# Gate/up blocks of a feed-forward group: two plain blocks replaced, six blocks started with the products that need no token differences

## The chip, the cores and the metric

The kernel runs on one core of one Trainium2 chip. The metric is the device time of one execution in microseconds (us). TensorE (PE) multiplies matrices and writes PSUM, VectorE (DVE) and ScalarE (ACT) work element by element, GpSimd (POOL) does little here, SyncE (SP) issues the loads. Each engine takes its instructions in the order of the built program.

## The reference, cut to what matters

One layer of a transformer step over 640 tokens (128 context, 512 latent) with width 1024. After attention, convolution and the output projection the layer ends in a SwiGLU feed-forward part with 2816 inner columns:

```python
h2 = _rms(x, norm_ffn) * (1 + sc2) + sh2
gate, up = jnp.split(h2 @ w_gate_up, 2, axis=-1)
x = x + g2 * ((jax.nn.silu(gate) * up) @ w_down)
```

All of it is float32.

## The kernel before, in words

**Precision.** Each float32 operand is kept as a high and a low part. `split` (L150) makes the high part on ScalarE and the low part on VectorE; `mm3` (L154) issues three matmuls for each product of two such operands (high x high, high x low, low x high).

**Tiling of gate/up.** The 2816 inner columns are 22 blocks f of 128, in four groups (`GCUT`, 6 + 6 + 5 + 5). For each block there are a gate weight "g" and an up weight "u", both 1024 x 128. A product here means 512 inputs x 128 columns x 320 tokens, 12 matmuls in `prod`. Let A11, A12 be the two input halves of g, A21, A22 those of u, and B11, B21 the two input halves of h2 for the first 320 tokens (LO), B12, B22 for the other 320 (HI). A *plain* block needs 8 products. A block by the Strassen-Winograd scheme needs 7: A11 B11, A12 B21, S1 T1, S2 T2, S3 T3, S4 B22, A22 T4. Here S1 = A21 + A22, S2 = S1 - A11, S3 = A11 - A21, S4 = A12 - S2 are sums of weights, and T1 = B12 - B11, T2 = B22 - T1, T3 = B22 - B12, T4 = B21 - T2 are differences between token halves. Blocks 0 and 1 are plain (`NPLAIN` = 2), all others take 7 products.

**Functions.** `plain` (L1183) runs the 8 products of a plain block: 4 on LO, later 4 on HI. `ff_a` to `ff_e` (L1215 to L1248) run the 7 products of the others: `ff_a` A11 B11, `ff_c` S1 T1, `ff_d` S2 T2, `ff_b` A12 B21, `ff_e` S3 T3, S4 B22, A22 T4. Partial results go from one PSUM bank to another, or to SBUF ("u2", "p5"), by a ScalarE copy. `ff_end` finishes the HI half, `ff_out` splits the result into the tile "gT" for the down product. `down` (L1256) runs a group's down product in two column halves; in group 0 it also runs the steps of the second half of the gate vector g2 (`g2_step`, VectorE) on four loads of w_ada.

**Where the h2 parts come from.** The output projection's loop ends with `h2_turn` (L1006): PE transposes a token block, ScalarE writes it to SBUF. For the last token block this stands inside block 0's products. `b_plain` and `b_put` (L1066) split a part of h2, `b_sums` (L1080) makes T1 to T4 and splits them, in two blocks of tokens of a half (0 to 192 and 192 to 320; before: 128 to 320 and 0 to 128).

**What sets the order.** PE's order is written out by hand. VectorE's order is written out between `dve_order.__enter__` and `__exit__`; instructions from outside may still be put between. All else is placed by a scheduler by priority (`early`). Weights stream through a list: `plan` (L188) puts loads and splits in order, and `W` (L259), called by each product, works that list up to 6 entries ahead (`AOP`). A raw load goes to one of three buffers "wf" (`WFB`), its parts to one of four "wh" and "wl" (`WHB`); a load is issued on SP when its buffer is free. `PRODS` gives the order of a block's splits, `PAIRS` says which tile holds which operand. `SEQ` (L39) is the hand-written order of the attention; in it S, T and O are attention steps, F1 is a piece of convolution, and r0 to r4 are `att_rms` (L952), two small matmuls on a sum that GpSimd has made.

Of the kernel before, what the change touches and what calls it, by code (L numbers as in the profile page):

```python
# [15 lines left out]
P = 128  # L16
# [33 lines left out]
GCUT = [0, 6, 12, 17, 22]  # L50
GB = 3
# [4 lines left out]
AOP = 6  # L56
NPLAIN = 2
PPO = ''
# [33 lines left out]
def build(ctx, tc, x_prompt, x_sample, c, cache_k, cache_v, c_ctx, norm_mix, norm_ffn, w_ada, b_ada,  # L92
# [101 lines left out]
    def op_load(e):  # L194

        f, name = e[0][1:]
        g, u = (order[place[x, f]][5] for x in "gu")
        a11, a12, a21, a22 = g[:, 0:4], g[:, 4:8], u[:, 0:4], u[:, 4:8]
        if name[0] == "S":
            if name == "S12":  # L200
                sums[f] = T("sx", (P, 8, P), F32, 2)
            s13, s24 = sums[f][:, 0:4], sums[f][:, 4:8]
            with early(SOP[f >= NPLAIN]):
                for out, x, y, op in {"S12": ((s13, a21, a22, ALU.add), (s24, s13, a11, ALU.subtract)),
                                      "S34": ((s13, a11, a21, ALU.subtract), (s24, a12, s24, ALU.subtract))}[name]:
                    dve.tensor_tensor(out, x, y, op)
            src = sums[f]
        else:
            src = {"A1": g, "A2": u, "A22": a22}[name]
# [6 lines left out]
        with early(SOP[f >= NPLAIN]):  # L216
            split(*e[5], src)
# [37 lines left out]
    def load_next(later=False):  # L255
        load(order[stream_at[0]], later)
        stream_at[0] += 1

    def W(key):  # L259
        p = place[key]  # L260
        while not in_pre[0] and stream_at[0] < len(order):
            nxt = order[stream_at[0]][0][0]
            ahead = AO if nxt == "o" else AOP if nxt in ("g", "u", "op") else AHEAD
# [28 lines left out]
    PAIRS = {"A11": ("A1", 0), "A12": ("A1", 4), "A21": ("A2", 0), "A22": ("A2", 4),  # L292
             "S1": ("S12", 0), "S2": ("S12", 4), "S3": ("S34", 0), "S4": ("S34", 4)}
# [764 lines left out]
    def b_tile(name):  # L1058
        w = T("gT" if name == "B12" else name, (P, 2, 4, HALF), F32R, GB if name == "B12" else 1)
        B[name] = [(w[:, 0, i], w[:, 1, i]) for i in range(4)] + [w]  # L1060
# [18 lines left out]

    def b_sums(part):  # L1080
        n = part.stop - part.start
# [8 lines left out]
        diff("T2", b22, w["T1"])  # L1090
        b_put("T1", w["T1"], part)
        diff("T3", b22, b12)
        b_put("T2", w["T2"], part)
        diff("T4", b21, w["T2"])
        b_put("T3", w["T3"], part)
        b_put("T4", w["T4"], part)
# [73 lines left out]
    open_pool("Y2", "left", "B22 T1 T2 T3 T4")  # L1170
    open_pool("G", "right", "cg cu p5 u2 dm tr")
    gT, st, pair = {}, {}, [None]
# [4 lines left out]
    def prod(out, f, a, b, start=True, stop=True, more=False):  # L1177
        x, k0 = PAIRS[a] if f < NPLAIN or a != "A22" else (a, 0)
# [4 lines left out]
    def plain(f, bs, toks, mid=None):  # L1183

        ps = [FB(), FB()]
        for x, a in zip(ps, ("A1", "A2")):
            for i in (1, 2):
                if mid is not None and (a, i) == ("A2", 2):
                    mid()
                prod(x, f, f"{a}{i}", bs[i - 1], i == 1, i == 2)  # L1190
        if toks is LO:
            st[f] = T("cg", (P, TOK), F32, 2), T("cu", (P, TOK), F32, 2)
        cg, cu = st[f]
        act.activation(cg[:, toks], ps[0][:, :HALF], AF.Silu)
        dve.tensor_tensor(cu[:, toks], ps[1][:, :HALF], cg[:, toks], ALU.mult)
        if toks is HI:
            ff_out(f, cu)
            del st[f]

# [9 lines left out]
    def copy_of(tag, ps):  # L1209
# [3 lines left out]
        return x  # L1213

    def ff_a(f):  # L1215
        b1, b2 = FB(), FB()
        prod(b1, f, "A11", "B11")
        with early(CPP):
            act.activation(b2[:, :HALF], b1[:, :HALF], AF.Copy)
        st[f] = [b1, b2, T("cg", (P, TOK), F32, 2), None, None, None]  # L1220

    def ff_b(f):
        b2, cg = st[f][1:3]
        prod(b2, f, "A12", "B21", start=False, more=True)
        act.activation(cg[:, LO], b2[:, :HALF], AF.Silu)

# [9 lines left out]
    def ff_e(f):  # L1236
        b1, _, cg, b3, p5, u2 = st[f]
        prod(b1, f, "S3", "T3", start=False, more=True)
        b4 = FB()
        with early(CPP):  # L1240
            act.activation(b4[:, :HALF], b1[:, :HALF], AF.Copy)  # L1241
# [4 lines left out]
        dve.tensor_tensor(cu[:, LO], b4[:, :HALF], cg[:, LO], ALU.mult)  # L1246
        st[f] = cg, cu, b3, u2

    def ff_end(f):
        cg, cu, b3, u2 = st.pop(f)  # L1250
        dve.tensor_tensor(cg[:, HI], b3[:, :HALF], u2, ALU.add)
        act.activation(cg[:, HI], cg[:, HI], AF.Silu)
        dve.tensor_tensor(cu[:, HI], cu[:, HI], cg[:, HI], ALU.mult)
        ff_out(f, cu)

    def down(gi, grp):  # L1256
        last = gi == len(GROUPS) - 1
        blocks = [grp[i:i + 2] for i in range(0, len(grp), 2)]
        for j in range(2):
# [23 lines left out]
            for t in range(NT):  # L1283
                cc = 1 if t == CTX else 0
                for part in acc[t]:
# [7 lines left out]
                    if last:  # L1293
                        sp.dma_start(o_dram[t][:, oc], x2[t][:, oc])

    for gi, grp in enumerate(GROUPS):
        for f in grp:
            if f == 0:
                dve_order = tc.manual_schedule(engines={mybir.EngineType.DVE})
                dve_order.__enter__()  # L1300
                b_plain("B12 B22", slice(0, 192))
                for x in range(NPLAIN):
                    plain(x, ("B11", "B21"), LO, None if x else lambda: h2_turn(TORD[-1], BPL))
                    if x == 0:
                        with early(BPL):
                            b_plain("B12 B22", slice(192, HALF))
                        b_sums(slice(128, HALF))
                        for _ in range(4):
                            load_next()
                b_sums(slice(0, 128))  # L1310
                dve_order.__exit__(None, None, None)
                phase[0] = 3
                for x in range(NPLAIN):
                    plain(x, ("B12", "B22"), HI)
            elif f >= NPLAIN:
                ff_a(f)
                if f - 1 in st and FEND == 1:
                    ff_end(f - 1)
                ff_c(f)
# [3 lines left out]
                ff_b(f)  # L1323
                ff_e(f)
                if f == grp[-1] or FEND == 0:
                    ff_end(f)
        down(gi, grp)
# [54 lines left out]
```

## Time and profile before

| | us |
|---|---|
| median of 3 runs | 755.55 (754.55 to 755.95) |
| the profiled execution | 756.18 |
| its span in the profile | 754.4 |
| VectorE busy | 530.2 (70%) |
| ScalarE busy | 374.9 (50%) |
| gate/up of group 0 in the span | 320.22 to 401.52 |

The span runs from the first to the last instruction in the profile; the execution's own time has 1.8 us around it. A time in a row of the profile counts from the span's start. Busy time of PE does not say that PE works at its peak, since matmuls overlap: their price is read from the step between two starts. The granted clock of TensorE is full over the whole span.

### The profile page before, as it was taken

To read this page: it belongs to the slowest core of one execution; us is meant where nothing else is said; L and a number is where in the kernel's file an instruction comes from. 1 tells how busy PE (TensorE), PEld (TensorE's weight loads), DVE (VectorE), ACT (ScalarE), POOL (GpSimd) and SP (SyncE) were. 2 spreads that over 40 slices of the span, in tenths; PEclk is the share of its full clock that TensorE was granted. 3 is DMA by queue.
4 is the path that set the end of the run, shared out by engine and by line. 5 is a ranking of instruction groups with operands and counts; after the bars stand their busy time and mean duration, and the time that the engine had idled before them with its cause. 6 is when DMAs were issued, how large, how long until landed. Compare 5 with 4: busy or idle time off the path is not lost.

```text
span 754.4 us, 11635 instructions
## 1 busy us (share of the span) xinstructions
PE 732.7 (97%) x4556; PEld 657.7 (87%) x4556; DVE 530.2 (70%) x905; ACT 374.9 (50%) x701; POOL 49.5 (7%) x85
## 2 busy tenths in 40 slices
PE   7999999999989999999899999999999999999997
PEld 5568878988988887899898799999889998899986
DVE  5558878676656798787868768774568766677653
ACT  5356777677666534775552225553125551255510
POOL 2403101011010120100000000000000000000000
PEclk9999999999999999999999999999999999999999
DMA  9985133533522464031225313233112232123312
GB/s 289 288 244 163 45 109 100 167 93 93 173 92 91 133 226 137 1 112 48 87 91 181 113 56 97 72 99 125 56 56 84 84 112 83 45 72 110 99 70 84
DMA packets 101387, 84.50 MB, mean 112 GB/s; under 512 B 3502, under 2 KB 81650, under 8 KB 101332
## 3 DMA queue, kind: packets, MB, share of 16 engines
q1 hardware_dynamic: 100980, 83.39, 35.9%
q0 software_dynamic: 352, 0.37, 0.3%
q8 instruction: 36, 0.59, 0.3%
q14 instruction: 19, 0.16, 0.1%
HBM read 79.68 MB, written 2.75 MB: 109 GB/s over the span
## 4 chain that ended last, share of the span: by engine, by line
PE 78%; DVE 7%; DMA 6%; ACT 5%; issue 2%; SPq 1%; POOL 1%; ACTq 0%; DVEq 0%
PE pf L155 17%; PE pf L156 17%; PE pf L157 17%; PE pc L723 3%; PE pc L724 3%; PE pc L725 3%; PE ps L835 2%; PE po L879 2%; PE pt L862 2%; DMA es<-t 2%; PE pc L394 2%; DMA af<-in_w_ada_dram 2%; DMA wf<-in_w_gate_up_dram 1%; PE ph L156 1%; PE ph L157 1%
## 5 line engine op out<-in xcount | busy, mean ns | idle before, releaser
L152 DVE TENSOR_TENSOR wl<-wf,wh 128x1024 fp32r<-128x1024 f32 (+1 forms) x58 | 68.7, 1185 | 59.1 <-ACT wh L151 44.6
L151 ACT ACTIVATE wh<-wf 128x1024 fp32r<-128x1024 f32 (+1 forms) x68 | 65.6, 968 | 86.2 <-PE pf L157 45.6
L155 PE MATMUL pf<-B,wh 128*128 128x320 f32 x288 | 89.3, 310 | 0.0
L157 PE MATMUL pf<-B,wl 128*128 128x320 f32 x288 | 89.3, 310 | 0.0
L156 PE MATMUL pf<-B,wh 128*128 128x320 f32 x288 | 89.2, 310 | 0.0
L155 PE MATMUL pf<-T,wh 128*128 128x320 f32 x280 | 86.9, 310 | 2.2 <-ACT pf L1241 1.6
L155 PE MATMUL pf<-wh,gT 128*128 128x512 f32 (+1 forms) x225 | 87.0, 387 | 0.0
L157 PE MATMUL pf<-T,wl 128*128 128x320 f32 x280 | 86.7, 310 | 0.0
L156 PE MATMUL pf<-T,wh 128*128 128x320 f32 x280 | 86.7, 310 | 0.0
L156 PE MATMUL pf<-wl,gT 128*128 128x512 f32 (+1 forms) x225 | 86.6, 385 | 0.0
L157 PE MATMUL pf<-wh,gT 128*128 128x512 f32 (+1 forms) x225 | 86.6, 385 | 0.0
L151 ACT ACTIVATE wh<-sx 128x1024 fp32r<-128x1024 f32 x40 | 42.4, 1060 | 82.9 <-PE pf L157 49.8
L152 DVE TENSOR_TENSOR wl<-sx,wh 128x1024 fp32r<-128x1024 f32 x40 | 48.9, 1224 | 27.4 <-ACT wh L151 23.8
L723 PE MATMUL pc<-hH,wh 128*128 128x320 f32 x192 | 61.2, 319 | 0.0
L724 PE MATMUL pc<-hL,wh 128*128 128x320 f32 x192 | 59.4, 309 | 0.0
L725 PE MATMUL pc<-hH,wl 128*128 128x320 f32 x192 | 59.4, 309 | 0.0
L155 PEld LDWEIGHTS pf<-T,wh 128*128 128x128 f32 x280 | 52.6, 188 | 2.7 <-ACT pf L1241 1.8
L157 PEld LDWEIGHTS pf<-B,wl 128*128 128x128 f32 x288 | 54.1, 188 | 0.1
L155 PEld LDWEIGHTS pf<-B,wh 128*128 128x128 f32 x288 | 54.1, 188 | 0.1
L156 PEld LDWEIGHTS pf<-B,wh 128*128 128x128 f32 x288 | 54.1, 188 | 0.1
L156 PEld LDWEIGHTS pf<-T,wh 128*128 128x128 f32 x280 | 52.6, 188 | 0.0
L157 PEld LDWEIGHTS pf<-T,wl 128*128 128x128 f32 x280 | 52.6, 188 | 0.0
(302 smaller groups left out, 1672.2 us busy)
## 6 DMA issues: line engine op xcount, KB each, us to landing
wf<-in_w_gate_up_dram SPq DMA_DIRECT2D x44, 512.0 KB, 3.8
aw<-in_w_ada_dram SPq DMA_DIRECT2D x24, 512.0 KB, 3.9
wf<-in_w_down_dram SPq DMA_DIRECT2D x20, 512.0 KB, 3.9
wf<-in_w_in_dram SPq DMA_DIRECT2D x18, 512.0 KB, 6.1
af<-in_w_ada_dram SPq DMA_DIRECT2D x32, 256.0 KB, 6.4
x<-in_x_sample_dram SPq DMA_DIRECT2D x8, 512.0 KB, 6.1
wf<-in_w_out_dram SPq DMA_DIRECT2D x8, 512.0 KB, 4.2
wf<-in_w_ada_dram SPq DMA_DIRECT2D x8, 512.0 KB, 3.8
```

What stands on the lines that cost most here:

```text
L151: act.activation(hi, src, AF.Copy)
L152: dve.tensor_tensor(lo, src, f32(hi), ALU.subtract)
L155: pe.matmul(out, lh, rh, start=start, stop=False, skip_group_check=more)
L156: pe.matmul(out, lh, rl, start=False, stop=False, skip_group_check=more)
L157: pe.matmul(out, ll, rh, start=False, stop=stop, skip_group_check=more)
L394: pe.matmul(out[CG * g:CG * (g + 1)], cp[:, k], w, start=(k < 4), stop=(k >= KD - 4), skip_group_check=True)
L723: pe.matmul(acc, wh[:, k], hH[k][:, c0:c0 + n], start=(k == 0), stop=False)
L724: pe.matmul(acc, wh[:, k], hL[k][:, c0:c0 + n], start=False, stop=False)
L725: pe.matmul(acc, wl[:, k], hH[k][:, c0:c0 + n], start=False, stop=(k == KD - 1))
L835: pe.matmul(s2[:, g, :320], q, kk[:, v, P + g * 320:P + (g + 1) * 320], start=(i == 0), stop=(i == 1))
L862: pe.transpose(tp[:, i, h], u[3][h][:, kt * P:(kt + 1) * P], ident)
L879: pe.matmul(ov, w, x[:, i].rearrange("p a q -> p (a q)"), start=(g == 0 and i == 0 and n == 0), stop=(last and i == len(kts) - 1 and n == 1))
```

## The change

Blocks 0 and 1 are no longer plain. For the six blocks of group 0 (`NDEF` = 6) the products that need no token differences (A11 B11 and A12 B21) run first, one block after the other; their results go to SBUF (in the buffers of "gT" that B12 held, and in a new tile "cgx"). Then, block by block, the other five products run, S2 T2 first, on a PSUM bank that ScalarE has filled again from SBUF (`seed`). The gate weight of these blocks is loaded twice ("g" for A1, and "G" for the sums). The weights' splits come in the order S12, A22, S34 for all blocks. B12 is no longer split. `b_sums` takes tokens 0 to 192 first, with weight loads between its steps, and `W` loads nothing ahead by itself meanwhile (`hold`). In `SEQ`, r0 and r2 stand later.

```diff
-       ... O5.0 T5.2 O5.1 F1 F1 Q2 O5.2 q3 r0 S7.0 F1 T6.0 T6.1 F1 T6.2 O6.0 S7.1 F1 F1 F1 O6.1 ...
+       ... O5.0 T5.2 O5.1 F1 F1 Q2 O5.2 q3 S7.0 F1 T6.0 T6.1 F1 T6.2 O6.0 S7.1 F1 F1 F1 r0 O6.1 ...
-       ... F1 F1 r2 O12.2 S14.0 T13.0 T13.1 F1 S14.1 F1 F1 T13.2 F1 O13.0 F1 O13.1 S15.0 F1 F1 O13.2 S15.1 T14.0
+       ... F1 F1 O12.2 S14.0 T13.0 T13.1 F1 S14.1 F1 F1 T13.2 F1 O13.0 F1 O13.1 S15.0 F1 F1 O13.2 S15.1 r2 T14.0
...
-    PLAIN, PRODS = ("A1", "A2"), ("A1", "S12", "S34", "A22")
+    PRODS = ("S12", "A22", "S34")
...
         for f in grp:
+            if f < NDEF:
+                plan_raw(f, "g", 2)
+                plan_ops(f, ("A1",), 2)
+        for f in grp:
+            if f < NDEF:
+                plan_raw(f, "G")
+            else:
+                plan_raw(f, "g")
+            plan_raw(f, "u")
+            plan_ops(f, PRODS if f < NDEF else ("A1",) + PRODS)
...
+    def def_a(f):
+        b1 = FB()
+        prod(b1, f, "A11", "B11")
+        k = store(f)
+        with early(CPP):
+            act.activation(k[:, 1], b1[:, :HALF], AF.Copy)
+        st[f] = b1
+
+    def def_b(f):
+        b1 = st.pop(f)
+        prod(b1, f, "A12", "B21", start=False, more=True)
+        act.activation(kept_f[f][:, 0], b1[:, :HALF], AF.Silu)
+
+    def def_c(f):
+        k = kept_f[f]
+        b1, b3 = FB(), FB()
+        seed(b1, k[:, 1])
+        prod(b1, f, "S2", "T2", start=False, more=True)
+        u2 = copy_of("u2", b1)
+        prod(b3, f, "S1", "T1")
+        st[f] = [b1, None, (k[:, 0], k[:, 1]), b3, copy_of("p5", b3), u2]
...
+    hold[0] = True
+    dve_order = tc.manual_schedule(engines={mybir.EngineType.DVE})
+    dve_order.__enter__()
+    b_plain("B22", slice(0, 192))
+    def_a(0)
+    def_a(1)
+    def_b(0)
+    h2_turn(TORD[-1], BPL)
+    loads_of(2)
+    b_sums(slice(0, 192), lambda: loads_of(2), lambda: loads_of(2))
+    with early(BPL):
+        b_plain("B22", slice(192, HALF))
+    for x in range(2, NDEF + 1):
+        if x < NDEF:
+            def_a(x)
+        def_b(x - 1)
+    b_sums(slice(192, HALF), lambda: loads_of(3), lambda: None)
+    dve_order.__exit__(None, None, None)
+    hold[0] = False
+    phase[0] = 3
...
-                plain(x, ("B12", "B22"), HI)
-            elif f >= NPLAIN:
+            if f < NDEF:
+                def_c(f)
+                if f:
+                    ff_end(f - 1)
+            else:
                 ff_a(f)
...
+            ff_e(f)
+            if f == grp[-1]:
+                ff_end(f)
```

More of the change, by code (lines that the diff above doesn't have):

```diff
@@ L56 @@
 AOP = 6
-NPLAIN = 2
+NDEF = 6
 PPO = ''
@@ L196, in op_load @@
         f, name = e[0][1:]
-        g, u = (order[place[x, f]][5] for x in "gu")
-        a11, a12, a21, a22 = g[:, 0:4], g[:, 4:8], u[:, 0:4], u[:, 4:8]
+        g = order[place["G" if f < NDEF and name != "A1" else "g", f]][5]
+        a11, a12 = g[:, 0:4], g[:, 4:8]
+        if name != "A1":
+            u = order[place["u", f]][5]
+            a21, a22 = u[:, 0:4], u[:, 4:8]
         if name[0] == "S":
@@ L202, in op_load @@
             s13, s24 = sums[f][:, 0:4], sums[f][:, 4:8]
-            with early(SOP[f >= NPLAIN]):
+            with early(SOP[f >= NDEF]):
                 for out, x, y, op in {"S12": ((s13, a21, a22, ALU.add), (s24, s13, a11, ALU.subtract)),
@@ L208, in op_load @@
         else:
-            src = {"A1": g, "A2": u, "A22": a22}[name]
+            src = g if name == "A1" else a22
         if name == "A22":
@@ L215, in op_load @@
             e[5] = T("wh", (P, 8, P), F32R, WHB), T("wl", (P, 8, P), F32R, WHB)
-        with early(SOP[f >= NPLAIN]):
+        with early(SOP[f >= NDEF]):
             split(*e[5], src)
@@ L1078, in b_plain, with b_sums @@
             b_put(x, quarter(x, part), part)
-    def b_sums(part):
+    def b_sums(part, *between):
         n = part.stop - part.start
@@ L1091, in b_sums @@
         b_put("T1", w["T1"], part)
+        between[0]()
         diff("T3", b22, b12)
@@ L1094, in b_sums @@
         diff("T4", b21, w["T2"])
+        between[1]()
         b_put("T3", w["T3"], part)
@@ L1170, in build @@
     open_pool("Y2", "left", "B22 T1 T2 T3 T4")
-    open_pool("G", "right", "cg cu p5 u2 dm tr")
+    open_pool("G", "right", "cg cu p5 u2 dm tr cgx")
     gT, st, pair = {}, {}, [None]
@@ L1181, in prod @@
             mm3(out[:, :HALF], wh[:, k0 + k], wl[:, k0 + k], *B[b][k], start and k == 0, stop and k == 3, more)
[L1183 to L1198, printed above, removed]
     def ff_out(f, cu):
@@ L1213, in copy_of, with seed, store @@
         return x
+    def seed(dst, src):
+        with early(CPP):
+            act.activation(dst[:, :HALF], src, AF.Copy)
+    kept_f = {}
+    def store(f):
+        if f == 0:
+            w = T("gT", (P, 4, 2, HALF), F32, GB)
+            kept_f.update({x: w[:, x] for x in range(4)})
+        elif f >= 4:
+            kept_f[f] = T("cgx", (P, 2, HALF), F32, 2)
+        return kept_f[f]
+    def def_a(f):
+        b1 = FB()
+        prod(b1, f, "A11", "B11")
+        k = store(f)
+        with early(CPP):
+            act.activation(k[:, 1], b1[:, :HALF], AF.Copy)
[12 more added lines that the diff above has]
+        st[f] = [b1, None, (k[:, 0], k[:, 1]), b3, copy_of("p5", b3), u2]
     def ff_a(f):
@@ L1217, in ff_a @@
         prod(b1, f, "A11", "B11")
-        with early(CPP):
-            act.activation(b2[:, :HALF], b1[:, :HALF], AF.Copy)
-        st[f] = [b1, b2, T("cg", (P, TOK), F32, 2), None, None, None]
+        seed(b2, b1[:, :HALF])
+        cg = T("cg", (P, TOK), F32, 2)
+        st[f] = [b1, b2, (cg[:, LO], cg[:, HI]), None, None, None]
     def ff_b(f):
@@ L1239, in ff_e @@
         b4 = FB()
-        with early(CPP):
-            act.activation(b4[:, :HALF], b1[:, :HALF], AF.Copy)
+        seed(b4, b1[:, :HALF])
         cu = T("cu", (P, TOK), F32, 2)
@@ L1294, in down, with loads_of @@
                         sp.dma_start(o_dram[t][:, oc], x2[t][:, oc])
+    def loads_of(n):
+        for _ in range(n):
+            load_next()
+    hold[0] = True
[18 more added lines that the diff above has]
+    phase[0] = 3
     for gi, grp in enumerate(GROUPS):
         for f in grp:
[L1298 to L1313, printed above, removed]
-                    plain(x, ("B12", "B22"), HI)
-            elif f >= NPLAIN:
+            if f < NDEF:
[3 more added lines that the diff above has]
+            else:
                 ff_a(f)
-                if f - 1 in st and FEND == 1:
-                    ff_end(f - 1)
                 ff_c(f)
```

28 lines of the change are left out of this document (11 added, 17 removed), and 8 rows, old and new, of the table SEQ.

## The prediction

> **What bounds the kernel now.** First the page's table of busy time, then the windows view cut where the gate/up work of group 0 begins and ends (the change works in there), then TensorE's own rows.
>
> ```profile
> span 754.4 us, 11635 instructions
> PE 732.7 (97%) x4556; PEld 657.7 (87%) x4556; DVE 530.2 (70%) x905; ACT 374.9 (50%) x701; POOL 49.5 (7%) x85
> ...
> 320.22:401.52 81.30, 79.08 (x540) 78.40 (x539) 64.60 (x91) 45.95 (x82) 0.54 (x1) 1.00 0.31 93
> 401.52:754.40 352.88, 348.91 (x2025) 322.57 (x2023) 236.17 (x330) 129.04 (x199) 0.00 (x0) 1.00 0.28 87
> ```
>
> TensorE (PE) is the bound: 97% busy, and in the stage that changes 79.08 of 81.30 us. VectorE (DVE) has 64.60 us of work there, 16.7 us of room. So time comes off only where TensorE runs fewer matmuls or waits less, and a change that spends VectorE's room can open new waits. TensorE's rows (start, duration, last column: idle before and who ended it):
>
> ```profile
> 155.26 0.35 PE L954 MATMUL pt<-ones,osq 128*128 128x1 f32 x2
> ...
> 225.64 0.38 PE L954 MATMUL pt<-ones,osq 128*128 128x1 f32 x2 [1.86 <-POOL osq L906]
> ...
> 320.22 0.39 PE L155 MATMUL pf<-B,wh 128*128 128x320 f32 x1
> ...
> 322.51 0.31 PE L157 MATMUL pf<-B,wl 128*128 128x320 f32 x1
> ...
> 326.76 0.31 PE L156 MATMUL pf<-B,wh 128*128 128x320 f32 x1
> 329.99 0.31 PE L157 MATMUL pf<-B,wl 128*128 128x320 f32 x1
> ...
> 361.80 0.41 PE L155 MATMUL pf<-T,wh 128*128 128x320 f32 x1 [1.59 <-ACT pf L1241]
> 371.50 0.41 PE L155 MATMUL pf<-T,wh 128*128 128x320 f32 x1 [0.64 <-ACT u L1212]
> ...
> 401.52 0.39 PE L155 MATMUL pf<-wh,gT 128*128 128x512 f32 x1
> 421.72 0.40 PE L157 MATMUL pf<-wh,gT 128*128 128x512 f32 x1
> ```
>
> Durations overlap, so the price of a matmul is the step between starts. From 326.76 to 329.99 are 22 steps: 0.147 us each, 1.76 us for a product of 12. From 401.52 to 421.72 are 89 steps of the down product's 90: 0.227 us.
>
> **What goes.** (1) Two plain blocks of 8 products become blocks of 7: 24 matmuls fewer (the built programs list 4116 and 4092 rows on PE), 24 x 0.147 = 3.5 us. (2) The two waits of 1.59 and 0.64 us stand in this stage; its order is new, so I take both away (2.2 us) and add all new waits below. (3) r2 moves 18 places later in the order of the attention work, past the wait for GpSimd at 225.64: 1.86 us, at worst nothing, if PE then meets the softmax sooner. r0, at 155.26, waited for nothing where it was. Together 7.6 us.
>
> **What comes.** Gate weights of six blocks are loaded twice; blocks 0 and 1 add sums of weights (S12, S34, A22 for A2). All of this lies on VectorE, ScalarE and the loads. The question is when the first product with differences (S2 T2 of block 0) finds its operands. PE is there after 12 products and the transposes: 320.22 + 12 x 1.76 + 1.0 = 342.4, later by any wait on the way. The rows that price VectorE and ScalarE:
>
> ```profile
> 322.10 1.22 DVE L152 TENSOR_TENSOR wl<-wf,wh 128x1024 fp32r<-128x1024 f32 x1
> ...
> 324.10 0.75 DVE L1162 TENSOR_SCALAR x2n<-x,rs 128x1024 f32<-128x1024 f32 x1 [0.66 <-POOL rs L1160]
> ...
> 327.24 2.36 DVE L152 TENSOR_TENSOR wl<-wf,wh 128x1024 fp32r<-128x1024 f32 x2
> ...
> 332.20 0.96 DVE L1087 TENSOR_TENSOR tr<-gT,tr 128x768 f32<-128x768 f32 x1
> 333.08 0.96 DVE L1074 TENSOR_TENSOR T<-tr,T 128x768 fp32r<-128x768 f32 x1
> ...
> 343.82 1.22 DVE L152 TENSOR_TENSOR wl<-sx,wh 128x1024 fp32r<-128x1024 f32 x1 [0.60 <-ACT wh L151]
> ...
> 347.17 0.68 DVE L1074 TENSOR_TENSOR T<-tr,T 128x512 fp32r<-128x512 f32 x1
> 347.77 0.68 DVE L1087 TENSOR_TENSOR tr<-gT,gT 128x512 f32<-128x512 f32 x1
> ```
>
> ```profile
> 326.24 0.42 ACT L1194 ACTIVATE cg<-pf 128x320 f32<-128x320 f32 x1
> 326.55 2.90 ACT L1020 ACTIVATE gT<-pt,modB,modA 128x128 f32<-128x128 f32 x8
> 329.29 0.68 ACT L1073 ACTIVATE gT<-gT 128x512 fp32r<-128x512 f32 x1
> ...
> 332.20 0.85 ACT L1073 ACTIVATE T<-tr 128x768 fp32r<-128x768 f32 x1 [1.71 <-DVE tr L1087]
> ...
> 342.72 1.06 ACT L151 ACTIVATE wh<-sx 128x1024 fp32r<-128x1024 f32 x1 [2.35 <-DVE sx L206]
> ...
> 369.38 0.74 ACT L151 ACTIVATE gT<-cu 128x640 fp32r<-128x640 f32 x1 [1.42 <-DVE cu L1253]
> ```
>
> Steps between VectorE starts: 1.14 us for a low part of 1024 (2.36 - 1.22), 0.87 for 768, 0.60 for 512, some 0.4 for 320. On ScalarE: 0.96 for 1024, 0.75 for 768, 0.32 for 320. A low part starts some 0.05 us after its high part ends.
>
> The order of the built program on VectorE, from the first block of differences (tokens 0 to 192 of a half) on:
>
> ```
> B22lo(0:192) A1_3lo dT1 dT2 T1lo A1_4lo dT3 T2lo dT4 A1_5lo T3lo T4lo B22lo(192:) | dT1 dT2 T1lo
> S12_0 sums, lo  A22_0lo  S34_0 sums  dT3 T2lo  S34_0lo  dT4  S12_1 sum1  T3lo  S12_1 sum2  T4lo ...
> ```
>
> Each engine takes its work in this order. I step through it on the clock of the profile. Up to 324 nothing moves, but PE's second product now needs the low part of A1_1, written from 322.10 to 323.3, and PE comes to its third matmul at 322.5 (the row at 322.51): a wait of 0.8 us. A third weight's low part goes ahead of x2n: x2n at 324.5, B22lo to 326.1, A1_3lo to 327.2, dT1, dT2 to 328.9, T1lo (behind its high part) to 330.0. ScalarE then does the high part of A1_4 (to 330.0), only then the 8 evictions of the last turned token block (2.90, to 332.8; before at 326.55), then a copy, the rest of B22, a Silu, the high part of A1_5 and at 334.9 that of T2 (to 335.7). VectorE stands from 332.1 to 335.8 at T2lo, 3.7 us, with dT4 and A1_5lo queued behind. From there: dT4 337.6, A1_5lo 338.7 (PE's sixth A11 waits 0.5 us), T3lo 339.6, T4lo 340.4, B22lo 341.1, dT1 dT2 T1lo 343.0, S12_0 sums 344.2, its low part 345.45 to 346.6, A22_0 347.2, S34_0 sums 348.4, dT3 349.0, **T2lo 349.7**. S2 T2 of block 0 needs that with its second matmul. PE came at 343.7 (342.4 + 0.8 + 0.5), so it waits 6 us.
>
> After it 30 products without a wait end at 349.75 + 30 x 1.76 = 402.6. Against that stands the chain of loads: in the built program every u lies in one and the same of the three wf buffers, so u of block f+1 is issued only when the first S34 sum of block f has read it. Issues on SP and the VectorE instructions that waited for them:
>
> ```profile
> 352.26 0.37 SPq L228 DMA_DIRECT2D wf<-in_w_gate_up_dram  x1
> 357.90 0.69 DVE L206 TENSOR_TENSOR sx<-wf 128x512 f32<-128x512 f32 x1 [2.02 <-DMA wf<-in_w_gate_up_dram]
> 364.35 0.37 SPq L228 DMA_DIRECT2D wf<-in_w_gate_up_dram  x1
> 368.25 0.69 DVE L206 TENSOR_TENSOR sx<-wf 128x512 f32<-128x512 f32 x1 [0.25 <-DMA wf<-in_w_gate_up_dram]
> 374.61 0.37 SPq L228 DMA_DIRECT2D wf<-in_w_gate_up_dram  x1
> 379.21 0.69 DVE L206 TENSOR_TENSOR sx<-wf 128x512 f32<-128x512 f32 x1 [1.27 <-DMA wf<-in_w_gate_up_dram]
> ...
> 404.75 2.29 SPq L228 DMA_DIRECT2D wf<-in_w_ada_dram  x2
> 408.61 5.57 DVE L1043 SCALAR_TENSOR_TENSOR cg<-wf,cs,cg 128x512 f32<-128x512 f32 x8 [0.39 <-DMA wf<-in_w_ada_dram]
> ...
> wf<-in_w_gate_up_dram SPq DMA_DIRECT2D x44, 512.0 KB, 3.8
> ```
>
> From issue to use: 5.64, 3.90, 4.60 and 3.86 us, the page's median landing 3.8. I take 4.1 (between the median and the mean of these rows, 4.5, nearer the median). A turn of the chain: 4.1 + two sums 1.3 + ScalarE's high part 1.1 + low part 1.2 + A22 0.6 + a sum 0.7 = 9.0, and 9.85 in every second turn, where an eviction of 0.4 and a copy or split on ScalarE (0.42, 0.74) come between: 9.5 on the mean, against 8.8 of PE for 5 products. PE starts with some 2 us in hand (S12_1 is split at 356.2, wanted at 358.6), so five turns cost it only 0.7 us at the end: **gate/up ends at 403.3** (401.52 before). The sums of S34_5 end at 395.9.
>
> The last piece is the down product, with the split of its third weight (w_down of blocks 4 and 5, "d2") in VectorE's rows and a windows row:
>
> ```profile
> 403.50 1.23 DVE L152 TENSOR_TENSOR wl<-wf,wh 128x1024 fp32r<-128x1024 f32 x1 [1.09 <-ACT wh L151]
> ...
> 401.52:445.00 43.48, 43.48 (x193) 35.49 (x192) 34.31 (x49) 8.69 (x9) 0.00 (x0) 1.00 0.36 112
> ```
>
> d2 was split by 404.7 before, 5 us ahead of its first use. In the new order it stands behind the steps of the second gate vector: four ada loads, each in a buffer that the gate/up work or the load before it frees. First load issued 395.4, used 399.45; two steps, a third, the split of block 4, a fourth step, d0lo, d1lo: 404.75. Second load issued at 402.6 when the first is read, used 406.7; two steps, four evictions, two steps, the split of block 5: 411.4; four steps on the third load (0.69 each, from the 5.57 us of eight): 414.1; **d2lo to 415.3**. PE wants d2 in its 38th matmul, 403.5 + 37 x 0.227 = 411.9, and waits 3.4 us. The same matmul ran at 401.52 + 37 x 0.227 = 409.9 before. Up to 445 VectorE has 43.48 - 34.31 = 9.2 us of room, so I add no further wait.
>
> **The sum.** 415.3 - 409.9 = +5.4, less 1.86 for r2: **+3.5 us** (by terms: -3.5 -2.2 -1.9; new waits 0.8 + 0.5 + 6.0 + 0.7 + 0.2 + 3.4 = 11.6; the rest is rounding). On the profiled execution's 756.18 that is 759.7; it lies 0.6 above the median of the runs, 755.55, so **759.1**.
>
> [...]
>
> **The rivals.**
> *Quick loads (within 0.2%)*. If loads take 3.7 us (the median less 0.1), each of the seven in a row to d2lo saves 0.4: d2lo at 412.5, +2.6, with r2 +0.7: 756.3. For it: the median; against: 4.60 and 5.64 in this very stage, and now u and the next G are issued together. [...]
> *Slow loads*. At 4.6, as in the row at 379.21, 7 x 0.5 = +3.5 more: 762.6.
> *VectorE is ahead (faster)*. One mechanism, at T2lo: if ScalarE has the high part of T2 when VectorE comes there (332.1), the 3.7 us go, and if the chain ends by 343.7 the whole 6. From there d2lo is early by as much: 415.3 - 6 = 409.3, -0.6, with r2 -2.5: 753.1; were d2 then on time as well, 749.5. It decides when T2lo ends 4 us or more before 349.7. Against it: ScalarE's order, in which 8 evictions and two splits stand ahead of T2.
> *The change doesn't do all it says*: r2's 1.86 us comes back as a wait for ScalarE in the attention: 761. Inside my range.
>
> **How the numbers follow.** Forecast with its neighbours (r2 kept or not, loads 3.9 to 4.4): 0.56, 757.1 to 762. Slow loads 0.13. Quick loads 0.17. VectorE ahead 0.14. About 0.2% (1.5 us) is what a measurement of this kernel can tell from no change. Faster 0.14, same 0.17, slower 0.69. The range leaves out half of the faster case and the far end of slow loads: 753.5 to 764.5.
>
> **What would show it.** PE: idle of 5 to 7 us before its first matmul on T2, ended by VectorE's T2 (right) or under 2 us (VectorE ahead); idle of 2 to 5 us in the first down product, ended by d2's low part; no 1.86 us before L954's place. VectorE: idle of some 3.7 us before the first T2lo. SP: w_gate_up issues every 9 to 10 us in pairs, 4.1 us to use. I am wrong if the waits before T2 and d2 are under half of that, or if new waits stand after 445.

## The result, and the profile after

The changed kernel takes 759.5 us (median of 4 runs, 758.5 to 760.0), the kernel before on the same chip 755.05 us (753.9 to 756.0). The ratio is 1.0057, 95% interval 1.0042 to 1.0072: slower by more than a measurement of this kernel leaves open. The forecast was 759.1. The profiled execution took 760.03 us, its span 758.2.

The page's table of busy time, and the windows view cut where gate/up of group 0 begins and ends in the changed kernel (columns as before: length, then busy time and count of PE, its weight loads, DVE, ACT, POOL, the granted clock, DMA share, GB/s):

```profile
span 758.2 us, 11640 instructions
PE 732.9 (97%) x4532; PEld 655.9 (86%) x4532; DVE 538.1 (71%) x919; ACT 380.7 (50%) x717; POOL 49.9 (7%) x85
...
318.66:404.59 85.93, 78.56 (x516) 76.45 (x514) 72.48 (x103) 51.60 (x97) 1.46 (x1) 0.98 0.41 119
404.59:758.20 353.61, 349.37 (x2025) 322.42 (x2023) 236.41 (x330) 129.39 (x200) 0.00 (x0) 1.00 0.29 89
```

The stage starts 1.56 us earlier than before (318.66 against 320.22: the wait at r2 is gone) and lasts 85.93 us instead of 81.30. With 24 matmuls fewer, TensorE's idle time in it rose from 2.2 to 7.4 us. VectorE's work in the stage went from 64.6 to 72.5 us, and its idle time there fell from 16.7 to 13.45 us. And the granted clock, 1.00 before, is 0.98. The rest of the span is 353.6 us against 352.9. So everything happened in this stage and at its end. TensorE's rows there that have idle time (last column: how long, and who ended it), and r2:

```profile
237.64 0.28 PE L965 MATMUL pt<-ones,osq 128*128 128x1 f32 x2
...
321.81 0.42 PE L157 MATMUL pf<-B,wl 128*128 128x320 f32 x1 [0.71 <-DVE wl L152]
324.34 0.41 PE L155 MATMUL pf<-B,wh 128*128 128x320 f32 x1 [0.80 <-ACT gT L1230]
342.24 0.42 PE L155 MATMUL pf<-B,wh 128*128 128x320 f32 x1 [0.93 <-ACT cgx L1230]
348.61 0.41 PE L156 MATMUL pf<-T,wh 128*128 128x320 f32 x1 [3.86 <-DVE T L1085]
...
380.88 0.42 PE L155 MATMUL pf<-T,wh 128*128 128x320 f32 x1 [0.56 <-ACT u L1208]
392.17 0.42 PE L155 MATMUL pf<-B,wh 128*128 128x320 f32 x1 [0.44 <-ACT p L1208]
...
413.82 0.50 PE L156 MATMUL pf<-wl,gT 128*128 128x512 f32 x1 [0.66 <-DVE wl L152]
```

Three of these were forecast: the wait of 0.71 us for the low part of A1_1, the long one before S2 T2 of block 0 (348.61), the one for d2 in the down product (413.82). The other four end on ScalarE's copies. The rows at 324.34 and 342.24 are A12 B21 products (of blocks 0 and 5): they go on in the PSUM bank out of which ScalarE has still to copy A11 B11 (L1230). The two later ones are of the same kind: S3 T3 goes on in the bank that is copied to "u2", S4 B22 in the one copied to "p5" (the profile's u and p). Block 5's copy did not lack time on ScalarE. It stood in ScalarE's order behind two splits for which ScalarE had waited for VectorE:

```profile
340.51 1.36 ACT L1084 ACTIVATE T<-tr 128x512 fp32r<-128x512 f32 x2 [2.21 <-DVE tr L1098]
341.77 0.42 ACT L1230 ACTIVATE cgx<-pf 128x320 f32<-128x320 f32 x1
```

VectorE's rows that answer to the steps of the forecast: the first T2lo, the first S34 sum of block 0, T2lo of the second token block, the first S34 sum of block 5, and d2's low part. The last line is the page's row of the loads.

```profile
334.57 0.96 DVE L1085 TENSOR_TENSOR T<-tr,T 128x768 fp32r<-128x768 f32 x1 [3.54 <-ACT T L1084]
...
346.07 0.68 DVE L209 TENSOR_TENSOR sx<-wf,wf 128x512 f32<-128x512 f32 x1
...
347.87 0.68 DVE L1085 TENSOR_TENSOR T<-tr,T 128x512 fp32r<-128x512 f32 x1
...
393.05 0.69 DVE L209 TENSOR_TENSOR sx<-wf,wf 128x512 f32<-128x512 f32 x1
...
412.56 1.21 DVE L152 TENSOR_TENSOR wl<-wf,wh 128x1024 fp32r<-128x1024 f32 x1
...
wf<-in_w_gate_up_dram SPq DMA_DIRECT2D x50, 512.0 KB, 4.4
```

On this clock, which is 1.56 us earlier, the forecast had VectorE idle for 3.7 us at the first T2lo (here 3.54), T2lo done at 348.1 (here 348.55), a turn of 9.5 us from one S34 sum to the next (here (393.05 - 346.07) / 5 = 9.4) and d2's low part done at 413.7 (here 413.77). Loads land in 4.4 us at the median, 3.8 before. But they are issued in pairs, and of the pair at 374.64 the first lands in 4.0 us and the second in 5.0. The chain goes by the first, u: from the issue of u on SP to VectorE's first use of it are 3.90, 3.76, 3.90, 3.99 and 4.46 us in the five turns, and 4.02 and 4.52 us for the two loads for g2 behind them. The mean of the seven is 4.1, which is what the forecast took. The last two turns of the chain, with the waits that a load ended:

```profile
378.63 0.69 DVE L209 TENSOR_TENSOR sx<-wf 128x512 f32<-128x512 f32 x1 [0.70 <-DMA wf<-in_w_gate_up_dram]
379.24 0.48 DVE L1277 TENSOR_TENSOR cu<-pf,gT 128x320 f32<-128x320 f32 x1
...
388.76 0.69 DVE L209 TENSOR_TENSOR sx<-wf 128x512 f32<-128x512 f32 x1 [0.77 <-DMA wf<-in_w_gate_up_dram]
```

```profile
379.76 0.74 ACT L151 ACTIVATE gT<-cu 128x640 fp32r<-128x640 f32 x1 [3.13 <-DVE cu L1277]
380.41 0.42 ACT L1208 ACTIVATE u<-pf 128x320 f32<-128x320 f32 x1
...
390.21 1.06 ACT L151 ACTIVATE wh<-sx 128x1024 fp32r<-128x1024 f32 x1 [1.12 <-DVE sx L209]
```

What the forecast did not have stands in the windows view, two microseconds each, behind the wait:

```profile
346.00:348.00 2.00, 0.00 (x0) 0.00 (x0) 2.00 (x5) 0.61 (x1) 0.00 (x0) 1.00 0.02 7
348.00:350.00 2.00, 1.39 (x7) 1.39 (x8) 2.00 (x3) 0.96 (x2) 0.00 (x0) 0.83 0.96 286
350.00:352.00 2.00, 2.00 (x10) 2.00 (x9) 1.59 (x4) 1.07 (x2) 0.00 (x0) 0.50 0.95 231
352.00:354.00 2.00, 2.00 (x13) 2.00 (x13) 1.42 (x4) 1.30 (x2) 0.00 (x0) 0.82 0.00 0
354.00:356.00 2.00, 2.00 (x16) 2.00 (x15) 2.00 (x3) 0.97 (x4) 0.00 (x0) 1.00 0.00 0
```

TensorE is busy from 348.6 on, yet it starts 10 matmuls in the third window where the last has 16: after the wait its granted clock is half, for about 3.4 us (2 x 2 x (0.17 + 0.50 + 0.18)), and 13 steps, from 349.30 to 352.74, take 0.24 to 0.27 us instead of 0.147. That lost 1.5 us.

**A ledger.** Call *lost* what the steps between neighbouring matmuls of gate/up and the first down product, from 318 to 460, have beyond 0.147 us (0.227 for 512 columns), where it is over 0.06. It holds waits, the slow clock and the 0.1 us that TensorE loses when it starts again after a wait (a first step of 0.25 us instead of 0.147, as from 321.81 to 322.06). Before it is 3.7 us, after 12.5. If TensorE's own row of work is all that sets the end, the span less the lost time, less what the kernels differ in by plan (24 matmuls, 3.5 us; r2's wait, 1.9 or 2.1; extra matmuls), must be one number. Over all profiled kernels of this study:

| kernel | span | lost | other | rest |
|---|---|---|---|---|
| before | 754.4 | 3.7 | 3.5 + 1.9 | 745.3 |
| after | 758.2 | 12.5 | | 745.7 |
| e1 | 750.9 | 1.9 | 3.5 | 745.5 |
| e2 | 757.7 | 12.4 | | 745.3 |
| e3 | 761.3 | 15.7 | | 745.6 |
| e4 | 760.6 | 15.0 | | 745.6 |
| e5 | 756.1 | 10.7 | | 745.4 |
| e6 | 754.6 | 9.3 | | 745.3 |
| e7 | 760.5 | 13.0 | 2.1 | 745.4 |
| e8 | 757.1 | 9.5 | 1.8 | 745.8 |
| e9 | 753.2 | 7.6 | | 745.6 |
| e10 | 751.9 | 2.3 | 3.5 | 746.1 |

It is, within 0.8 us. So the change saved 3.5 + 1.9 and lost 12.5 - 3.7 = 8.8 more, +3.4 by the ledger and +3.8 in the span. The ledger says where the time went; it does not say what made TensorE lose it, nor which loss would come back elsewhere if it were taken away. The open question was what makes TensorE lose that time.

### The profile page after: what moved, and what is told of

Read it like the earlier page. It is cut to its first block, busy times and chain, and to the rows that moved or that the text cites. A ratio compares the mean times of both kernels' runs of the same rounds, so it can differ in the third digit from the quotient of the medians.

```text
span 758.2 us, 11640 instructions
## 1 busy us (share of the span) xinstructions
PE 732.9 (97%) x4532; PEld 655.9 (86%) x4532; DVE 538.1 (71%) x919; ACT 380.7 (50%) x717; POOL 49.9 (7%) x85
## 4 chain that ended last, share of the span: by engine, by line
PE 75%; DVE 9%; DMA 6%; ACT 5%; issue 3%; POOL 1%; SPq 1%; POOLq 0%; DVEq 0%; ACTq 0%
PE pf L156 17%; PE pf L157 17%; PE pf L155 16%; PE pc L734 3%; PE pc L735 3%; PE pc L736 3%; PE po L890 2%; PE pt L873 2%; PE ps L846 2%; PE pc L405 2%; DMA es<-t 2%; DVE wl L152 1%; PE ph L156 1%; PE ph L157 1%; DMA af<-in_w_ada_dram 1%
## 5 line engine op out<-in xcount | busy, mean ns | idle before, releaser
L156 PE MATMUL pf<-T,wh 128*128 128x320 f32 x308 | 95.9, 312 | 3.9 <-DVE T L1085 3.9
L155 PE MATMUL pf<-T,wh 128*128 128x320 f32 x308 | 96.1, 312 | 0.6 <-ACT u L1208 0.6
L157 PE MATMUL pf<-T,wl 128*128 128x320 f32 x308 | 95.9, 311 | 0.0
L155 PE MATMUL pf<-B,wh 128*128 128x320 f32 x264 | 82.2, 311 | 2.2 <-ACT cgx L1230 0.9
L157 PE MATMUL pf<-B,wl 128*128 128x320 f32 x264 | 81.8, 310 | 0.7 <-DVE wl L152 0.7
L156 PE MATMUL pf<-B,wh 128*128 128x320 f32 x264 | 81.6, 309 | 0.0
L152 DVE TENSOR_TENSOR wl<-sx,wh 128x1024 fp32r<-128x1024 f32 x44 | 53.9, 1225 | 31.0 <-ACT wh L151 27.4
L156 PEld LDWEIGHTS pf<-T,wh 128*128 128x128 f32 x308 | 58.4, 190 | 4.1 <-DVE T L1085 4.1
L155 PEld LDWEIGHTS pf<-T,wh 128*128 128x128 f32 x308 | 58.5, 190 | 1.3 <-ACT u L1208 1.0
L157 PEld LDWEIGHTS pf<-T,wl 128*128 128x128 f32 x308 | 58.4, 190 | 0.0
L155 PEld LDWEIGHTS pf<-B,wh 128*128 128x128 f32 x264 | 49.6, 188 | 3.2 <-ACT cgx L1230 1.2
L156 PEld LDWEIGHTS pf<-wl,gT 128*128 128x128 f32 x225 | 42.3, 188 | 9.6 <-DVE wl L152 1.1
L157 PEld LDWEIGHTS pf<-B,wl 128*128 128x128 f32 x264 | 49.5, 188 | 1.1 <-DVE wl L152 1.0
```

What stands on the lines that cost most here:

```text
L152: dve.tensor_tensor(lo, src, f32(hi), ALU.subtract)
L155: pe.matmul(out, lh, rh, start=start, stop=False, skip_group_check=more)
L156: pe.matmul(out, lh, rl, start=False, stop=False, skip_group_check=more)
L157: pe.matmul(out, ll, rh, start=False, stop=stop, skip_group_check=more)
```

## The experiments

Theory A: VectorE's chain (loads, S34 sums, d2's low part) sets when TensorE can end, so that a wait taken away elsewhere comes back at d2. Theory B: each of TensorE's losses counts by itself. The runs were made on several chips, so they are compared by their ratio to the kernel before on the same chip: the changed kernel stands at 1.0057, and 0.001 is 0.76 us.

**e1: the attention order alone.** The kernel before with the new `SEQ` (r0, r2 later) and nothing else.

> The kernel before with nothing but the later places of r0 and r2. Theory: the 1.86 us wait before r2 goes and nothing takes its place: 1.6 to 1.9 us faster than before, ratio 0.9976 to 0.9979. Rival (the wait comes back as a wait for ScalarE's softmax): ratio 1.000.

Measured: 752.78 us, ratio 0.9960 (0.9947 to 0.9974), -3.0 us, faster than both kernels and more than either value written down. r2 runs at 237.59 without a wait, as it does in the changed kernel. That is 1.9 of the 3.0. The rest is in gate/up: of the two waits of 1.59 and 0.64 us one of 0.90 is left.

```profile
368.02 0.42 PE L155 MATMUL pf<-T,wh 128*128 128x320 f32 x1 [0.90 <-ACT u L1212]
```

The ledger says the same (lost 1.9 us instead of 3.7). Why shifting the attention by 2 us also mends the gate/up stage stays open; e10 below, the same kernel once more, gives 2.3 us instead of 3.0.

**e2: d2 early.** The steps of g2's second half get a low priority, so that w_down's splits stand ahead of them on VectorE (the new line at the top moves all line numbers by one).

```diff
+G2L = -600
...
-              with early(G2P) if G2P and j == 0 else ExitStack():
+              with early(G2P if j == 0 else G2L):
```

> The changed kernel, with the steps of the second gate vector at a low priority, so that the splits of d2 and of block 5 stand four steps (2.75 us) earlier on VectorE. Theory A (VectorE's chain up to d2's low part sets the time, TensorE's waits ahead of it are covered): 2.7 us less than the changed kernel, 756.8. Theory B (TensorE's own losses ahead of it add up and bring it to d2 only 0.7 us before d2's low part): 0.7 us less, 758.8.

Measured: 759.16 us, ratio 1.0046 (1.0030 to 1.0062). The wait for d2 is gone from the trace, and 0.8 us with it by the two ratios, whose intervals overlap. The half clock lasted 6.8 us in the profiled execution instead of 3.4 (granted clock 0.72, 0.50, 0.50, 0.57 in the windows from 346 to 354; TensorE runs again from 348.38 on). On the first chip the ratio is 758.5 us: that is theory B's time, and theory A's 756.8 did not come. With TensorE only 0.66 us ahead of d2's low part, no more than that could come of d2 alone.

**e3: the differences ahead of the weights.** Two more weight loads are put behind the second block of differences, inside VectorE's hand-written order. T2lo then comes before the sums S34_0.

```diff
     b_sums(slice(192, HALF), lambda: loads_of(3), lambda: None)
+    loads_of(2)
     dve_order.__exit__(None, None, None)
```

> The changed kernel, with A22 and S34 of block 0 split behind the second block of differences instead of in front of it. T2's low part is then some 1.8 us earlier, and the wait of 3.9 us before the first product with T2 should be near 2. The first S34 sum, and with it the load of u of block 1, is 3 us later. Theory A (the chain of loads and d2 on VectorE sets the time): about 3 us slower than the changed kernel, 762.5. Theory B (the wait before T2 and TensorE's half clock after it set the time): 2 to 4 us faster, 755.5 to 757.5.

Measured: 762.97 us, ratio 1.0096 (1.0080 to 1.0112). The wait for T2 falls from 3.86 to 2.05 us, and the kernel gets 3 us slower. What was taken there comes back at once, and more:

```profile
346.83 0.56 PE L156 MATMUL pf<-T,wh 128*128 128x320 f32 x1 [2.05 <-DVE T L1085]
353.47 0.41 PE L155 MATMUL pf<-T,wh 128*128 128x320 f32 x1 [1.47 <-ACT wh L151]
354.73 0.41 PE L157 MATMUL pf<-T,wl 128*128 128x320 f32 x1 [0.70 <-DVE wl L152]
```

S34_0 is now late (its first sum at 349.29 instead of 346.07), S3 T3 of block 0 waits for it, and each later sum stands some 3 us behind: 396.65 for block 5 instead of 393.05. The sums are the links of VectorE's chain, and TensorE waits at d2 again, 3.2 us later than in the changed kernel:

```profile
417.00 0.50 PE L156 MATMUL pf<-wl,gT 128*128 128x512 f32 x1 [0.57 <-DVE wl L152]
```

Theory A had named this time.

**e4: the weights ahead of the differences.** The other way round: five weight loads instead of three ahead of the second T2.

```diff
-    b_sums(slice(192, HALF), lambda: loads_of(3), lambda: None)
+    b_sums(slice(192, HALF), lambda: loads_of(5), lambda: None)
```

> The changed kernel, with all weights of block 0 split in front of the second block of differences, S34's low part too. T2's low part is 1.2 us later, the wait before it near 5 us, the chain of loads stays where it is. Theory A: within 0.5 us of the changed kernel, 759.5 to 760. Theory B: 1.2 us slower or more, 760.7 to 761.5. In either, TensorE's steps after the wait should be at 0.27 us for some 4 us, as in the changed kernel.

Measured: 762.80 us, ratio 1.0093 (1.0077 to 1.0109). VectorE's first S12_1 sum, which waits for the load of u1 until 350.68, now stands ahead of T2lo, and TensorE waits 7.29 us for T2, until 352.02, where near 5 had been expected. Its clock is half for 6.8 us (0.83, then 0.50 three times, from 348 to 356), 2.7 us of that while it still waits. S34_0 is as early as in the changed kernel and d2 holds nobody; still the kernel is 2.7 us slower, more than theory B's 1.2 to 2. Here TensorE's own losses set the time. So neither theory holds alone: with e3 the chain was the later of the two, with e4 TensorE. In the changed kernel they meet at d2 with 0.7 us between them.

**e5: T2's high part first.** One edit in `b_sums`, on ScalarE: the high part of T2 goes ahead of the 8 evictions of the last token block. VectorE's order in that stretch stays as it was.

```diff
-        b_put("T2", w["T2"], part)
+        with early(2500): b_put("T2", w["T2"], part)
```

> One edit: in the first block of differences ScalarE makes the high part of T2 at once, ahead of the 8 evictions; VectorE's order there stays. VectorE's 3.5 us of idle before the first T2lo should go; 1.5 of it come back one place further on, because the evictions now end 0.9 us later and the high part of A1_5 with them, so T2lo of the second block ends at 346.5 instead of 348.5. The wait before S2 T2 falls from 3.9 to about 1.9 us, and if a long wait is what lowers the clock, the granted clock stays above 0.9 there. Theory A (VectorE's chain sets the end: everything on it comes 2.0 earlier, d2's low part at 411.8): 757.5 us. Theory B (TensorE's losses add up: 2.0 of the wait and 2.0 of the slow clock): 755.5 us. Neither: 759.5.

Measured: 758.01 us, ratio 1.0033 (1.0017 to 1.0048). VectorE's rows and then TensorE's:

```profile
330.80 0.95 DVE L1085 TENSOR_TENSOR T<-tr,T 128x768 fp32r<-128x768 f32 x1
334.11 1.23 DVE L152 TENSOR_TENSOR wl<-wf,wh 128x1024 fp32r<-128x1024 f32 x1 [1.49 <-ACT wh L151]
...
345.92 0.68 DVE L1085 TENSOR_TENSOR T<-tr,T 128x512 fp32r<-128x512 f32 x1
```

```profile
346.66 0.55 PE L156 MATMUL pf<-T,wh 128*128 128x320 f32 x1 [3.03 <-DVE T L1085]
...
411.84 0.50 PE L156 MATMUL pf<-wl,gT 128*128 128x512 f32 x1 [0.54 <-DVE wl L152]
```

The first T2lo waits for nobody (330.80 instead of 334.57), 1.49 us come back one place on at A1_5, T2lo of the second block ends at 346.6 and d2's low part 2.0 us earlier, all as written down. The wait before S2 T2 is 3.0 us and not 1.9, because TensorE came 1.0 us sooner (the copy wait at 342.24 is gone), and the clock, which was to stay above 0.9, fell to half for 3.4 us. The time is theory A's within 0.5 us; theory B's was 2.5 off. One thing speaks against reading this as theory A alone, see the last section: executions of this kernel without a fall of the clock are faster. The mechanism of the forecast's rival "VectorE is ahead" is real, and the edit of one line gets 1.8 of its 6 us.

**e6: VectorE ahead.** T2, T3 and T4 first on ScalarE, the split of A1_5 behind T4 on VectorE, d2 early as in e2.

```diff
-        b_put("T2", w["T2"], part)
+        with early(2500): b_put("T2", w["T2"], part)
...
-        b_put("T3", w["T3"], part)
-        b_put("T4", w["T4"], part)
+        with early(2500): b_put("T3", w["T3"], part)
+        with early(2500): b_put("T4", w["T4"], part)
...
-    b_sums(slice(0, 192), lambda: loads_of(2), lambda: loads_of(2))
+    b_sums(slice(0, 192), lambda: loads_of(2), lambda: None); loads_of(2)
```

> Three edits: the high parts of T2, T3 and T4 at once on ScalarE, the split of A1_5 behind T4 on VectorE, and the second gate vector's steps behind the splits of w_down (as in the run with d2 early). T2lo of the second block should end near 345.7, the wait before S2 T2 be 1 us, the clock full, and d2 cost nothing. Theory A (the chain of loads and S34 then sets the end: it gains 2.8 us from the start, d2 0.3): 756.5 us, with new waits of 1 us or so on weights in blocks 3 to 5. Theory B (TensorE's losses: 2.9 + 2.0 + 0.7): 754 us. A result under 752.8 would be the fastest version so far.

Measured: 756.07 us, ratio 1.0008 (0.9996 to 1.0020). The time is theory A's, but not for its reason. The wait for T2 is down to 0.32 us; a new one stands at another place:

```profile
334.55 0.41 PE L155 MATMUL pf<-B,wh 128*128 128x320 f32 x1 [2.25 <-ACT gT L1230]
347.37 0.41 PE L156 MATMUL pf<-T,wh 128*128 128x320 f32 x1 [0.32 <-DVE T L1085]
```

ScalarE's rows show why: the copy of A11 B11 (L1230), for which A12 B21 waits, now stands behind T3, T4 and B22.

```profile
331.75 1.17 ACT L1031 ACTIVATE gT<-pt,modB,modA 128x128 f32<-128x128 f32 x3
332.77 0.88 ACT L1084 ACTIVATE T<-tr 128x768 fp32r<-128x768 f32 x1
333.51 0.66 ACT L1084 ACTIVATE B<-gT 128x512 fp32r<-128x512 f32 x1
334.03 0.47 ACT L1230 ACTIVATE gT<-pf 128x320 f32<-128x320 f32 x1
```

**e7: the gate/up change without the attention order.** The changed kernel with the old `SEQ`.

> The changed kernel with the attention order of before (r0 and r2 where they stood): what the change of the gate/up blocks does by itself. Additive: the 1.86 us of r2 come back and nothing else, 761.4 us. If the 3.0 us that the new attention order gave alone belong to it in full, 762.5 us. If the end is set by something that does not shift with r2, 759.5 us.

Measured: 762.39 us, ratio 1.0088 (1.0069 to 1.0107). So the gate/up change by itself costs 0.88%, 6.6 us, and the attention order gives 0.31%, 2.3 us, of it back. The intervals are too wide to tell the 1.9 of "additive" from the 3.0 of e1. The spans say 2.3 as well (760.5 to 758.2), 2.1 of it the wait that returned:

```profile
225.71 0.38 PE L965 MATMUL pt<-ones,osq 128*128 128x1 f32 x2 [2.09 <-POOL osq L917]
```

**e8: TensorE kept busy.** The changed kernel with 12 more matmuls of 320 columns, which add nothing to the output, ahead of S2 T2. All other engines keep their order.

```diff
-    phase[0] = 3
+    phase[0] = 3; fill, fw = PB((P, 512)), W(("op", NDEF - 1, "A1"))[0]; [pe.matmul(fill[:, :HALF], fw[:, 0], B["B11"][0][0], start=True, stop=True) for _ in range(12)]
```

> The changed kernel with 12 more matmuls of 320 columns into an unused PSUM tile, ahead of block 0's S2 T2 (their result is read by nothing); VectorE's, ScalarE's and the loads' orders are the same as in the changed kernel. TensorE then stands 2.1 us before T2lo instead of 3.9. If the length of the wait is what lowers the clock, the granted clock from 350 to 352 is 0.8 or more instead of 0.50, and the loss of 2 us falls to 0.6 or less; time then 759.0 by theory A (d2's low part still comes at 413.8, so only 0.3 to 0.7 is gained) and 758.0 by theory B. If the clock falls for another reason (the work that starts there), it is 0.50 as before and the time 759.5.

Measured: 759.48 us, ratio 1.0048 (1.0029 to 1.0067; 7 runs, 757.4 to 760.2). First TensorE's row, then the windows behind it:

```profile
348.84 0.41 PE L156 MATMUL pf<-T,wh 128*128 128x320 f32 x1 [2.44 <-DVE T L1085]
```

```profile
348.00:350.00 2.00, 1.16 (x8) 1.16 (x9) 2.00 (x4) 1.19 (x2) 0.00 (x0) 1.00 0.81 234
350.00:352.00 2.00, 2.00 (x15) 2.00 (x15) 1.23 (x3) 0.96 (x2) 0.00 (x0) 1.00 1.08 285
```

With a wait of 2.44 instead of 3.86 us the clock stays full, under the same work and the same burst of loads. So the work that starts there and the loads don't lower the clock by themselves. That the shorter idle time kept it full is likely but not shown: this is one execution, and waits of 2.05 (e3) and 2.25 us (e6) were followed by a half clock. What the full clock gave in time can't be told either. The intervals allow anything from nothing to 2.5 us, and the profiled execution, 760.21 us with a span of 757.1, has 3.1 us around its span where the other profiled ones have 1.8 to 2.1.

**e9: the copies first.** e6, and ScalarE's copies of A11 B11 ahead of all else.

```diff
         k = store(f)
-        with early(CPP):
+        with early(3000):
```

> The kernel of the run e6 with one more edit: ScalarE's copies of A11 B11 (for which TensorE's A12 B21 of the same block waits in the same bank) come ahead of everything else it has. TensorE's waits of 0.8 and 2.25 us for these copies should go, and with the second the half clock from 335 to 338.7. TensorE's lost time between 318 and 460 falls from 9.3 to between 4.5 and 6.0 us, depending on how long it then stands before S2 T2 (0.3 to 1.5 us). If the span is 745.5 us plus that lost time, as it was in the kernels so far, it is 750.0 to 751.5 and the time 752 to 753.5. If a chain of loads or splits behind it holds the end instead, new waits of the same size appear in blocks 1 to 5 and the time stays at 756.

Measured: 755.09 us, ratio 0.9993 (0.9983 to 1.0002), the span 753.2. The wait of 2.25 us and the half clock went. The 752 to 753.5 us written down did not come. Lost time is 7.6 us, not 4.5 to 6.0: TensorE still waits for ScalarE's copies, 1.10 us at 324.62 and 0.72 at 342.31, 1.26 us for T2, and twice (0.67 and 0.54) for the eviction "p". This is the best form of the gate/up change that was found, and it is no faster than the kernel before.

**e10: e1 again**, on the same chip as e9.

> The kernel before with the new attention order alone, once more, on the same chip as the run above, for the comparison of the two fastest kernels: 752.8 us, or 0.9960 of the kernel before.

Measured: 753.01 us, ratio 0.9970 (0.9958 to 0.9981), -2.3 us. The intervals of e9 and e10 do not touch: the old gate/up with the new attention order is the fastest kernel of this study, 2 us ahead of e9.

## Why the prediction came out right, point by point

- **24 matmuls fewer, 3.5 us:** right. Without this term the ledger would be open by 3.5 us, with it it closes within 0.8.
- **r2, 1.86 us:** right for the wait itself (gone in e1 and in the changed kernel, back as 2.09 in e7). The attention order is worth some more, 2.3 us in e7, 3.0 in e1 and 2.3 in e10; the excess in e1 lies in the old gate/up waits. The changed stage itself starts 1.56 us earlier, not 1.86.
- **The old waits, 2.2 us:** they went, with new ones added as the forecast counted.
- **Low part of A1_1, 0.8:** 0.71. **The sixth A11, 0.5:** no such wait.
- **T2lo:** VectorE's walk was right within 0.5 us (349.7 less 1.56 is 348.1; 348.55 measured), the 3.7 us of idle behind the 8 evictions included (3.54; e5 removes it with one edit on ScalarE). **The wait before T2, 6 us:** 3.86. The step that failed is "PE is there after 12 products": it was there 2.2 us later, since A12 B21 of block 0 and of block 5 waited for ScalarE's copy out of their own PSUM bank (0.80 and 0.93 of idle time, 0.96 and 1.09 in the steps). The forecast had priced the copies' time on ScalarE, but not that the next product into the bank has to wait for them.
- **"After it 30 products without a wait end at ... 402.6":** wrong by 3 us. From T2 to the end of gate/up are 404.59 - 348.61 = 55.98 us, 52.85 forecast: 1.5 by the half clock, which the forecast did not have, 1.3 by the two waits for ScalarE's copies "u" and "p" (0.72 and 0.60 in the steps), the rest restarts. The chain of loads, for which 0.7 and 0.2 were put down, did reach TensorE, but by way of ScalarE. VectorE's waits for a load at 378.63 and 388.76 (0.70 and 0.77 us) made its next instructions late, and ScalarE's copies "u" and "p" stood behind work that waits for these. So by the rows the 1.3 us are the chain's; no run takes the loads' waits away. The turn of the chain was right (9.4 against 9.5).
- **d2, 3.4 us of wait:** 0.66. The time of d2's low part was right (413.7 and 413.77); TensorE was late for it by what it had lost more above.
- So the terms after T2 were wrong by 3 us up and by 3 down, and the sum held. That is in part luck, and in part not: while TensorE comes to d2 ahead of VectorE, its earlier losses are covered, and the end follows d2's low part, which VectorE's walk gave to 0.1 us. But the cover was nearly used up, 0.66 us were left. Had TensorE lost one microsecond more, the forecast by d2 would have been too low; e4 is that case. By the forecast's own signs one of its two waits failed: 3.86 us before T2 is above half of the 5 to 7 named, 0.66 at d2 is under half of 2 to 5.
- **The rivals.** Slow and quick loads did not occur: the seven loads in a row to d2lo took 4.1 us on the mean, not 4.6 or 3.7. What a slower or quicker load costs was not tested by itself. "VectorE is ahead" decided where it was placed, at the first T2lo (e5), but it gives 1.8 us for one edit and not 6, since other things on ScalarE become late. "r2 comes back" did not happen.

## What to carry to other kernels

Walk the engine with the least room left through its built order, to the last thing that the bound engine needs from it: that time was right to half a microsecond where the single waits were not. For the bound engine, add who reads a PSUM bank before the next product goes on in it (waits of 0.80 and 0.93 us here, for A12 B21 of blocks 0 and 5). And price the work that a reordering brings to the second and third engine against the matmuls that it saves: 3.5 us of matmuls cost 8.8 us of lost time here, and each of the edits e3 to e6, which moved work forward on VectorE or ScalarE, made something else on these engines late.

## What the runs showed of the hardware that was not expected

In these traces TensorE's granted clock falls to half in lumps, in gate/up each time in or behind a wait of 2.05 to 7.29 us. Summed over the windows (2 x (1 - clock) x length), it was half for 3.4 us in the gate/up stage of the changed kernel, e3, e5 and e6, and for 6.8 in that of e2, e4 and e7. The long waits there were 2.05 us (e3), 2.25 (e6), 3.03 (e5), 3.86 (after, e2), 3.85 (e7) and 7.29 (e4). No fall came there after 2.44 (e8) or 1.26 (e9). For e6 the windows, with TensorE busy again from 334.55:

```profile
332.00:334.00 2.00, 0.30 (x3) 0.04 (x1) 1.71 (x3) 2.00 (x5) 0.00 (x0) 1.00 0.55 165
334.00:336.00 2.00, 1.45 (x7) 1.45 (x8) 1.17 (x2) 2.00 (x6) 0.00 (x0) 0.82 0.00 0
336.00:338.00 2.00, 2.00 (x9) 2.00 (x9) 1.97 (x4) 0.85 (x4) 0.00 (x0) 0.50 0.04 11
338.00:340.00 2.00, 2.00 (x14) 2.00 (x13) 1.97 (x4) 0.67 (x3) 0.00 (x0) 0.83 0.88 258
```

A lump followed the 2.25 us there and none the 2.44 in e8, so the length alone does not decide. Two other places in the traces say the same. Behind r2's wait the clock fell for 3.4 us in e7 (2.09 us; steps of 0.27 us instead of 0.147 from 228.69 on) and not in the kernel before (1.86; the windows from 220 to 242 all have 1.00). And near the start, where TensorE waits 1.06 and then 0.38 us just ahead, five profiles (e2, e3, e5, e7, e8) have a lump of 3.4 us from about 19 us on, and seven, with the same two waits, have none:

```profile
17.35 0.50 PE L155 MATMUL ps<-wh,hH 128*128 128x512 f32 x1 [1.06 <-ACT hH L497]
18.23 0.50 PE L156 MATMUL ps<-wl,hH 128*128 128x512 f32 x1 [0.38 <-DVE wl L560]
```

These two rows are e5's. The early lump does not show in the ledger: the five kernels with it have a rest of 745.3 to 745.8, the others of 745.3 to 746.1. It does show in the mean granted clock of e8's profiled execution, 0.998 with a full clock in gate/up. Which waits of nearly the same length are followed by a lump and which are not, and why a lump lasts 3.4 us or twice that, no run shows.

What a fall costs in time is less clear than its 1.5 us of slow steps. Of the 12 executions of e5, 4 have a mean granted clock of 1.000 and take 756.3 to 757.3 us; the 8 others have 0.993 to 0.998 and take 757.9 to 760.0. By the medians, 756.7 and 758.3, these differ by 1.6 us. But the mean counts falls at any place, the profiled execution of e5 has the early lump too, and in the kernel before the mean clock varies from one execution to the next without such a split of the times. So this is a sign and no proof. If it holds, VectorE's chain alone did not set e5's end.
